# A Trainium2 kernel of two transformer blocks: the experts' outputs added to rows of x in DRAM by accumulating scatters

## The chip, the cores and the metric

The kernel runs on one core of one Trainium2 chip. The metric is the device time of one launch in microseconds (us); lower is better. Everything is float32 with float32-level accuracy: each product of a weight and an activation is made of three matrix multiplications of split operands (a rounded high part and the rest, the low part).

## The reference

Two blocks over one sequence of 512 tokens of width 1024. The first block is a mixer of three branches and then a hierarchical mixture of experts; the second block is attention, convolution, a memory attention and a feed-forward net. What is touched here is the end of the first block:

```python
def hier_moe(h, ...):                       # h: norm of x, 512 x 1024
    grp_prob = softmax(hf @ w_group + b_group);  p_g, g_idx = top_k(grp_prob, 1)      # 1 of 4 groups
    top_vals, e_idx = top_k(sel_logits, 2)                                            # 2 of its 4 experts
    weights = p_g * softmax(top_vals)
    for each expert e:  act = silu(hf @ w_gate[e]) * (hf @ w_up[e]) * combine[:, e];  y += act @ w_down[e]
x = x + gt2 * ffn        # end of the first block; the second block starts with rmsnorm(x)
```

So each token adds two experts' outputs, each times its own weight, to its row of x. There are 16 experts of hidden width 256.

## The kernel before

The tokens lie in four tiles of 128 (NT = 4). A planner holds all weight loads in the order of their use (`add_unit`, `fetch`): a load on SP's queue fills one of six raw buffers, ACT casts it to the high part, DVE (in the expert loop also Pool for some) subtracts to get the low part (`split_raw`, L212 and L215). A compiler pass orders the instructions of each engine and sets every semaphore; it also waits wherever two accesses to one tile, in DRAM too, must keep their order. Pages are 13 buffers of 128 x 2048 floats, shared by everything large.

*Up to the routing.* `wo_route` ends the mixer: it adds its output to x tile by tile, computes the norm for the experts, stores it to DRAM (`h2_d`, L1314) and computes the router's logits. x stays on the chip in two pages. Long before, `mixer` stores zeros to the last six of 24 blocks of `y_d` (L1224 to L1227).

*Routing.* `route` finds for each token its two experts, its two weights (`w12`) and its place: tokens of one expert get consecutive slots of a unit of 128 slots. There are 24 units; 18 are always worked on (one for each of 16 experts, two more for the experts that have over 128 tokens), six are spare. Matrix multiplications with one-hot operands turn places into a table that says which token sits in each slot of each unit (`slots`, L1515; empty slots name token 0), and `rowi` (L1497) says for each token at which rows of `y_d` its two outputs will lie.

*The expert loop.* `moe` visits the 18 units. For a unit, `gather` fetches 128 rows of `h2_d` by an indirect DMA on Pool's queue (L1532) into one of two buffers, TensorE transposes them (L1538), `expert_up` multiplies by the gate and up weights, `expert_down` by the down weights; a unit's `expert_down` stands in the program behind the next unit's `expert_up`. The result leaves PSUM on DVE, times the row gt2 (L1583, two halves of 128 x 512), into small buffers (tag `tmp`, five of them, used for other steps too), and SP stores each half to the unit's block of `y_d` (L1584).

*The branch.* Behind the 18 units stands a conditional (L1625) with the six spare units, which these inputs do not need. Each engine evaluates the branch; the queues of an engine whose DMAs were skipped bring their semaphores to the counts that the body would have left.

*The seam.* Eight indirect DMAs on Pool gather from `y_d` by token, 128 rows of 4 KB each, two for each tile of tokens (L1648). DVE multiplies each by its weight and adds it to x (L1652). After two tiles `fm_half` transposes x (L1715), scales it to the high and low parts (L1718, L1719) and computes the norm's factors (L1722 to L1731); then the other two tiles follow. Pool stores x to `x_d` (L1658); the second block loads it again from there some 250 us later (L2188). `self.mark`, the last L1652, is what two kinds of SP loads wait for at the start of the second block (the bias tables, L496, and one weight load, L183).

## Time and profile before

| | us |
|---|---|
| median of 3 runs | 1646.08 |
| lowest, highest | 1641.83, 1646.18 |
| the profiled execution, whole | 1647.19 |
| its span in the profile | 1645.2 |

The profile is of one execution. Busy shares of its span: TensorE 93%, DVE 64%, ACT 40%, Pool 16%. Its mean granted TensorE clock is 0.965 of full speed. A stretch's row tells the engines' busy time, the granted clock (1.00 is 2.4 GHz, 0.50 is 1.2 GHz) and the mean share of time in which the 16 DMA engines were busy. A row of waits names the waiting engine, the tile and the line, what ended the wait, the total, how often, and the longest. SyncE (SP) computes nothing, it issues DMAs.

### The profile page before, as it was taken

The page shows a single profiled execution, that of the slowest core. Times are in us where ns is not written, and L with a number is a line of the kernel's source. Part 1 is how long each engine was busy: PE and PEld are TensorE (multiplying, and loading weights), DVE is VectorE, ACT ScalarE, POOL GpSimd, SP SyncE. Part 2 cuts the span into 40 slices and gives each one's busy share as a digit, 9 for nine tenths or more (in the row PEclk, how much of TensorE's full clock was granted, in tenths as well). Part 3 has the DMA queues.
Part 4 walks back from the last instruction along what each step waited for, and adds up shares of the span by engine and source line. Part 5 has one row for each costly group of instructions (what it writes and reads, how often), then busy time and mean ns, then how long its engine had stood idle before and what let it go on. Part 6 is the DMA issues. An engine that isn't in the chain of part 4 may idle for free. (4 is left out here: it accounts for less than half of the span.)

```text
span 1645.2 us, 23279 instructions
## 1 busy us (share of the span) xinstructions
PE 1529.7 (93%) x8945; PEld 1289.3 (78%) x8945; DVE 1051.3 (64%) x2068; ACT 666.1 (40%) x1221; POOL 270.7 (16%) x294
## 2 busy tenths in 40 slices
PE   4999989999999999699985999999988999999998
PEld 3878867779988899588884886666766889889888
DVE  6797778755664466788986667777466541443445
ACT  6443434212342353555763444445455332331222
POOL 4032123110010000333323112112111110100010
PEclk9899999989999999799997989999999999999999
DMA  9334236324353324799995440113220223223221
GB/s 342 82 100 139 62 118 226 105 90 154 126 182 105 100 77 140 268 322 333 343 373 194 153 130 26 31 47 78 102 84 32 95 85 103 87 93 103 82 79 71
DMA packets 184118, 224.75 MB, mean 137 GB/s; under 512 B 11049, under 2 KB 161269, under 8 KB 184002
## 3 DMA queue, kind: packets, MB, share of 16 engines
q1 hardware_dynamic: 172432, 194.44, 35.7%
q0 software_dynamic: 7024, 26.48, 4.8%
q10 hardware_dynamic: 4546, 2.27, 0.6%
q8 instruction: 73, 1.20, 0.3%
q14 instruction: 43, 0.35, 0.1%
HBM read 204.27 MB, written 22.84 MB: 138 GB/s over the span
## 5 line engine op out<-in xcount | busy, mean ns | idle before, releaser
L238 PE MATMUL mm<-pg,whi 128*128 128x512 f32 (+1 forms) x968 | 380.6, 394 | 4.6 <-DVE pg L725 4.5
L239 PE MATMUL mm<-pg,whi 128*128 128x512 f32 (+1 forms) x968 | 379.0, 392 | 0.6 <-DVE pg L643 0.3
L240 PE MATMUL mm<-pg,wlo 128*128 128x512 f32 (+1 forms) x968 | 377.8, 391 | 0.0
L215 DVE TENSOR_TENSOR wlo<-wraw,whi 128x1024 fp32r<-128x1024 f32 (+3 forms) x204 | 239.6, 1186 | 211.0 <-ACT whi L212 209.9
L212 ACT CAST whi<-wraw 128x1024 fp32r<-128x1024 f32 (+3 forms) x210 | 200.2, 968 | 217.6 <-PE mm L239 119.9
L238 PE MATMUL mm<-whi,pg 128*128 128x256 f32 (+2 forms) x928 | 276.4, 298 | 6.4 <-ACT pg L857 3.1
L240 PE MATMUL mm<-whi,pg 128*128 128x256 f32 (+2 forms) x928 | 272.5, 294 | 0.0
L239 PE MATMUL mm<-wlo,pg 128*128 128x256 f32 (+2 forms) x928 | 272.3, 294 | 0.0
L238 PEld LDWEIGHTS mm<-pg,whi 128*128 128x128 f32 x968 | 185.5, 192 | 45.7 <-DVE pg L725 4.7
L239 PEld LDWEIGHTS mm<-pg,whi 128*128 128x128 f32 x968 | 185.7, 192 | 39.7 <-issue 2.1
L240 PEld LDWEIGHTS mm<-pg,wlo 128*128 128x128 f32 x968 | 185.9, 192 | 38.1 <-DVE wlo L215 0.8
L238 PEld LDWEIGHTS mm<-whi,pg 128*128 128x128 f32 x928 | 176.0, 190 | 13.5 <-ACT pg L857 3.3
L240 PEld LDWEIGHTS mm<-whi,pg 128*128 128x128 f32 x928 | 175.9, 190 | 4.7 <-DVE pg L274 0.6
L239 PEld LDWEIGHTS mm<-wlo,pg 128*128 128x128 f32 x928 | 176.1, 190 | 3.7
L2272 POOL TENSOR_TENSOR tmp<-tmp,bc 128x512 f32<-128x512 f32 x22 | 28.6, 1298 | 298.5 <-DVE tmp L2271 298.5
L436 DVE SCALAR_TENSOR_TENSOR tmp<-wraw,cact,tmp 128x256 f32<-128x256 f32 x112 | 57.0, 510 | 1.8
L2021 ACT ACTIVATE atmp<-atmp,nm 128x384 f32<-128x384 f32 (+3 forms) x64 | 34.9, 546 | 36.2 <-DVE nm L2019 25.0
L212 ACT CAST whi<-pg 128x1024 fp32r<-128x1024 f32 x36 | 36.3, 1052 | 19.0 <-PE mm L240 13.2
L239 PE MATMUL at<-wlo,pg 128*128 128x256 f32 x136 | 40.4, 297 | 3.6 <-DVE wlo L215 3.6
L238 PE MATMUL at<-pg,pg 128*128 128x256 f32 x152 | 43.7, 287 | 0.0
L215 DVE TENSOR_TENSOR wlo<-pg,whi 128x1024 fp32r<-128x1024 f32 x28 | 42.0, 1514 | 2.6 <-ACT whi L212 2.6
L239 PE MATMUL at<-pg,pg 128*128 128x256 f32 x152 | 43.3, 285 | 0.0
(557 smaller groups left out, 2632.1 us busy)
## 6 DMA issues: line engine op xcount, KB each, us to landing
wraw<-in_w_in_dram SPq DMA_DIRECT2D x34, 1024.0 KB
wraw<-in_w_mod_dram SPq DMA_DIRECT2D x16, 1024.0 KB
pg<-in_w_exp_gate_dram SPq DMA_DIRECT2D x14, 1024.0 KB
wraw<-in_ffn_wg_dram SPq DMA_DIRECT2D x11, 1024.0 KB
wraw<-in_ffn_wu_dram SPq DMA_DIRECT2D x11, 1024.0 KB
pg<-in_w_exp_down_dram SPq DMA_DIRECT2D x10, 1024.0 KB
y_d<-tmp SPq DMA_DIRECT2D x36, 256.0 KB
pg<-in_w_mod_dram SPq DMA_DIRECT2D x8, 1024.0 KB
```

The source lines that it names most:

```text
L212: cp = nc.scalar.copy(h, x)
L215: ins = eng.tensor_tensor(l, x, h.bitcast(F32), op=OP.subtract)
L238: nc.tensor.matmul(out, ah, bh, start=start, stop=False)
L239: nc.tensor.matmul(out, ah, bl, start=False, stop=False)
L240: nc.tensor.matmul(out, al, bh, start=False, stop=stop)
L436: nc.vector.scalar_tensor_tensor(t, w[:, k, :], self.cact[:, k:k + 1], t, op0=OP.mult, op1=OP.add)
L2021: nc.scalar.activation(lg[:, :n], lg[:, :n], AF.Exp, bias=nm, scale=-1.0, accum_out=den[:, c:c + 1])
L2272: nc.gpsimd.tensor_tensor(act[c], act[c], bc, op=OP.mult)
```

## The change

Six edits:

1. The zero stores and `y_d` go.
2. `wo_route` stores x, tile by tile on SP, to `x_d` before it stores the norm; the pages of x are given up there.
3. `route` keeps its eight one-hot tables in one page and uses them twice: for the token of each slot (now numbered from 1, so that 0 is an empty slot) and for the weight of each slot (`wslot`). From the former come `slots` as before and `dest`, the row of x for each slot, or a row beyond the end for an empty slot. `rowi` goes.
4. `expert_down` multiplies by gt2 and by the slot's weight in one operation per half, into one of two halves of a page (`yrows`), and one indirect DMA on Pool adds the 128 rows to the rows `dest` of `x_d`; rows beyond the end are skipped. Stores by SP go. The spare units do the same.
5. At the seam the gathers, the sums on DVE and Pool's store of x go. x is loaded from `x_d` on SP into two pages, and both calls of `fm_half` follow.
6. `self.mark` becomes the first L1719 operation of the second `fm_half`.

```diff
--- before.py
+++ after.py
@@ -1220,11 +1220,6 @@
         if not GFIRST:
             ya = self.gmlp(h, gc)
         self.gla_proj(h)
-
-        zero = self.t(self.lvp, [128, 1024], tag="lv")
-        nc.gpsimd.memset(zero, 0.0)
-        for u in range(18, NU):
-            nc.sync.dma_start(self.y_d[u * 128:(u + 1) * 128, :], zero)
         self.drain_bg()
         self.bg.append(self.gla_levels())
         self.pump(GP0)
@@ -1311,7 +1306,10 @@
             r = self.rstd(self.small, s1, D, 1, "rs2")
             nc.vector.scalar_tensor_tensor(self.L[:, i, :], pl[:, :20], r, self.br, op0=OP.mult, op1=OP.add)
             nc.vector.scalar_tensor_tensor(xs[i], xs[i], r, self.sh2r, op0=OP.mult, op1=OP.add)
+            nc.sync.dma_start(self.x_d[i * 128:(i + 1) * 128, :], self.x[i])
             nc.sync.dma_start(self.h2_d[i * 128:(i + 1) * 128, :], xs[i])
+
+        self.x = None
 
 
     def eid_value(self, table, u):
@@ -1335,11 +1333,15 @@
 
         self.iof, self.tok = iof[:, 0:128], iof[:, 128:132]
 
+        nc.vector.tensor_scalar(self.tok, self.tok, 1.0, None, op0=OP.add)
+
+        self.none = self.t(const, [128, 1], tag="none")
+        nc.vector.tensor_scalar(self.none, iof[:, 128:129], float(S), None, op0=OP.add)
+
         self.stri = self.t(const, [128, 128], tag="stri")
         nc.gpsimd.affine_select(out=self.stri, in_=self.ones, pattern=[[1, 128]], compare_op=OP.is_gt,
                                 fill=0.0, base=0, channel_multiplier=-1)
         self.h2_d = self.dram.tile([S, D], F32, name="h2_d")
-        self.y_d = self.dram.tile([128 * NU, D], F32, name="y_d")
         self.x_d = self.dram.tile([S, D], F32, name="x_d")
 
     def first_max(self, x, m, rev, out, shape):
@@ -1402,8 +1404,8 @@
         d = T("dd", NT)
         nc.vector.tensor_tensor(d, m2, m1, op=OP.subtract)
         nc.scalar.activation(d, d, AF.Exp)
-        self.w12 = self.t(self.const, [128, 2, NT], tag="w12")
-        w1, w2 = self.w12[:, 0], self.w12[:, 1]
+        w12 = T("w12", 2, NT)
+        w1, w2 = w12[:, 0], w12[:, 1]
         nc.vector.tensor_scalar(w1, d, 2.0, 2.0, op0=OP.mult, op1=OP.add)
         nc.vector.reciprocal(w1, w1)
         nc.vector.tensor_tensor(w1, w1, pg_, op=OP.mult)
@@ -1493,8 +1495,6 @@
             t = T("pick", NT, 16)
             nc.vector.tensor_tensor(t, O[c], unit, op=OP.mult)
             nc.vector.tensor_reduce(uc[:, c, :], t, axis=AX.X, op=OP.add)
-        self.rowi = self.t(self.const, [128, 2, NT], I32, tag="rowi")
-        nc.vector.scalar_tensor_tensor(self.rowi, uc, 128.0, sc_, op0=OP.mult, op1=OP.add)
 
         pt = self.ms()
         U4 = [128, 2, NT, 24]
@@ -1504,15 +1504,27 @@
         nc.vector.tensor_tensor(onu, uc.unsqueeze(3).to_broadcast(U4),
                                 self.iof[:, :24].unsqueeze(1).unsqueeze(1).to_broadcast(U4), op=OP.is_equal)
         nc.vector.tensor_tensor(tou, onu, self.tok.unsqueeze(1).unsqueeze(3).to_broadcast(U4), op=OP.mult)
+        Rp = self.page(F32R)
         for c in range(2):
             for i in range(NT):
-                R = self.t(self.small, [128, 512], F32R, tag="atmp", bufs=NATMP)
-                at, to = R[:, :128], tou[:, c, i, :]
+                q = NT * c + i
+                at, to = Rp[:, q * 128:q * 128 + 128], tou[:, c, i, :]
                 (nc.gpsimd if c < RP else nc.vector).tensor_scalar(at, self.iof, sc_[:, c, i:i + 1], None, op0=OP.is_equal)
-                q = NT * c + i
                 nc.tensor.matmul(pt[:, :24], at, to, start=q == 0, stop=q == 2 * NT - 1)
         self.slots = self.t(self.const, [128, NU], I32, tag="slots")
-        self.routed = nc.vector.tensor_copy(self.slots, pt[:, :NU])
+        self.routed = nc.vector.tensor_scalar(self.slots, pt[:, :NU], 1.0, 1.0, op0=OP.max, op1=OP.subtract)
+
+        dest = T("dest", NU)
+        self.after(nc.vector.tensor_scalar(dest, pt[:, :NU], 0.0, self.none, op0=OP.is_equal, op1=OP.mult), self.routed)
+        self.dest = self.t(self.const, [128, NU], I32, tag="dest")
+        nc.vector.scalar_tensor_tensor(self.dest, pt[:, :NU], -1.0, dest, op0=OP.add, op1=OP.add)
+        nc.vector.tensor_tensor(onu, onu, w12.unsqueeze(3).to_broadcast(U4), op=OP.mult)
+        pw = self.at()
+        for q in range(2 * NT):
+            nc.tensor.matmul(pw[:, :NU], Rp[:, q * 128:q * 128 + 128].bitcast(F32), onu[:, q // NT, q % NT, :], start=q == 0,
+                             stop=q == 2 * NT - 1)
+        self.wslot = self.t(self.const, [128, NU], tag="wslot")
+        nc.vector.tensor_copy(self.wslot, pw[:, :NU])
 
         eid = T("eid", 8)
         ef = T("ef", 6, 16)
@@ -1573,15 +1585,16 @@
         aT = self.t(self.small, [128, 512], F32R, tag="tmp", bufs=NTMP)
         self.split(aT[:, :256], aT[:, 256:], pt[:, :256])
         wh, wl = get("xd")
+        y = self.yrows[u % 2]
         for half in range(2):
             py = self.mm()
             hs = slice(half * 512, half * 512 + 512)
             for k in range(2):
                 self.mm3(py, aT[:, k * 128:(k + 1) * 128], aT[:, 256 + k * 128:256 + (k + 1) * 128],
                          wh[:, k, hs], wl[:, k, hs], k == 0, k == 1)
-            y = self.tmp()
-            nc.vector.tensor_tensor(y, py, self.gt2r[:, hs], op=OP.mult)
-            nc.sync.dma_start(self.y_d[u * 128:(u + 1) * 128, hs], y)
+            nc.vector.scalar_tensor_tensor(y[:, hs], py, self.wslot[:, u:u + 1], self.gt2r[:, hs], op0=OP.mult, op1=OP.mult)
+        nc.gpsimd.indirect_dma_start(out=self.x_d, out_offset=bass.IndirectOffsetOnAxis(ap=self.dest[:, u:u + 1], axis=0),
+                                     in_=y, in_offset=None, bounds_check=S - 1, oob_is_err=False, compute_op=OP.add)
 
     def moe(self):
         nc, tc, A = self.nc, self.tc, self.A
@@ -1590,6 +1603,8 @@
         self.ahead, self.limit = RAW + 2, self.order[("xd", UNITS[-1][1])] + LIM
         self.hold = self.routed
         self.mem_branch(*self.mem)
+        yp = self.page()
+        self.yrows = yp[:, :D], yp[:, D:]
         hT = self.gather(UNITS[0][0])
         self.hold = None
         uses, live = self.moe_order(), {}
@@ -1642,20 +1657,11 @@
                 self.expert_down(u, self.expert_up(self.gather(u, hroom), get), get)
         self.rooms = self.limit = None
         self.fm_begin()
-        pgs = [self.page() for _ in range(NT)]
-        for i in range(NT):
-            for c in range(2):
-                nc.gpsimd.indirect_dma_start(out=pgs[i][:, c * D:c * D + D], out_offset=None, in_=self.y_d,
-                                             in_offset=bass.IndirectOffsetOnAxis(ap=self.rowi[:, c, i:i + 1], axis=0))
-        for i in range(NT):
-            for c in range(2):
-                self.mark = nc.vector.scalar_tensor_tensor(self.x[i], pgs[i][:, c * D:c * D + D], self.w12[:, c, i:i + 1],
-                                                           self.x[i], op0=OP.mult, op1=OP.add)
-            if i % 2:
-                self.fm_half(self.nrm[0], i // 2, [pg[:, :D] for pg in pgs])
-
-        for i in range(NT):
-            nc.gpsimd.dma_start(self.x_d[i * 128:(i + 1) * 128, :], self.x[i])
+        self.x = self.load_x(nc.sync, self.x_d)
+        junk = self.tm_pages()
+        for hf in range(2):
+            self.mark = self.fm_half(self.nrm[0], hf, junk)
+
         self.x = None
 
 
@@ -1707,6 +1713,7 @@
 
         nc = self.nc
         hs = slice(hf * 256, hf * 256 + 256)
+        first = None
         for kk in range(4):
             pt = self.at() if kk % 2 else self.tp()
             for k in (2 * kk, 2 * kk + 1):
@@ -1716,8 +1723,9 @@
             for k in (2 * kk, 2 * kk + 1):
                 pk = pt[:, k % 2 * 256:k % 2 * 256 + 256]
                 nc.scalar.activation(self.fh[k][:, hs], pk, AF.Copy, scale=g[:, k:k + 1])
-                nc.vector.scalar_tensor_tensor(self.fl[k][:, hs], pk, g[:, k:k + 1], self.fh[k][:, hs].bitcast(F32),
-                                               op0=OP.mult, op1=OP.subtract)
+                q = nc.vector.scalar_tensor_tensor(self.fl[k][:, hs], pk, g[:, k:k + 1], self.fh[k][:, hs].bitcast(F32),
+                                                   op0=OP.mult, op1=OP.subtract)
+                first = first or q
         for i in (2 * hf, 2 * hf + 1):
             nc.scalar.activation(junk[i], self.x[i], AF.Square, accum_out=self.fms[:, i:i + 1])
         r = self.r[:, 2 * hf:2 * hf + 2]
@@ -1729,6 +1737,7 @@
             nc.vector.tensor_scalar(dg, self.ident, r[:, i:i + 1], None, op0=OP.mult)
             nc.tensor.matmul(pb[:, i * 128:(i + 1) * 128], self.ones, dg, start=True, stop=True)
         nc.scalar.copy(self.bc[:, hs], pb[:, :256])
+        return first
 
     def f2_halves(self, unit, evac):
 
```

## Rows read from the trace of the kernel before

**Rows 1.** Stretches: length, busy us of PE, PEld, DVE, ACT, POOL, clock, DMA, GB/s.
```profile
660.00:700.00 40.00, 23.83 (x163) 22.52 (x162) 31.55 (x81) 20.39 (x27) 12.50 (x8) 0.79 0.78 266
...
740.00:780.00 40.00, 37.89 (x266) 34.24 (x265) 33.80 (x43) 23.22 (x34) 13.16 (x7) 1.00 0.96 333
780.00:820.00 40.00, 38.32 (x269) 34.64 (x268) 38.56 (x48) 29.15 (x39) 13.19 (x8) 1.00 0.96 337
820.00:860.00 40.00, 37.23 (x260) 33.65 (x258) 34.22 (x41) 25.01 (x35) 12.20 (x5) 1.00 1.03 377
860.00:878.00 18.00, 13.94 (x73) 11.65 (x73) 13.61 (x16) 8.69 (x12) 3.10 (x2) 0.91 0.40 134
878.00:894.50 16.50, 0.00 (x0) 0.00 (x0) 6.20 (x7) 0.07 (x1) 6.47 (x7) 0.63 0.70 226
...
897.00:903.00 6.00, 6.00 (x29) 6.00 (x30) 5.08 (x9) 4.39 (x10) 2.11 (x4) 0.52 0.95 370
...
909.00:913.00 4.00, 3.43 (x26) 2.95 (x25) 3.84 (x11) 2.18 (x6) 2.77 (x6) 1.00 1.03 399
```

**Rows 2.** Waits, 640 to 930 us: engine, line, releaser: total us, times, longest.
```profile
POOL lv L1532 <- PE tp L1538: 88.0, 16, 9.2
...
PE tp L1715 <- DVE pg L1652: 18.0, 2, 16.6
...
PE tp L1538 <- DMA lv<-h_d,slots: 8.7, 2, 7.2
...
PE mm L240 <- DVE tmp L274: 7.6, 7, 2.0
...
ACT whi L212 <- DMA pg<-in_w_exp_gate_dram: 3.0, 1, 3.0
...
ACT pg L212 <- DMA pg<-in_w_exp_gate_dram: 2.3, 1, 2.3
```

**Rows 3.** Chain that ended last, around the seam: start us, length us, what.
```profile
885.50 0.70 issue
886.20 5.57 DMA pg<-y_d,rowi
...
895.63 1.30 DVE pg L1652
...
896.97 0.90 PE tp L1715 x3
```

**Rows 4.** Timeline of the seam: start us, length us, engine, line, operation.
```profile
877.97 1.29 DVE L1583 TENSOR_TENSOR tmp<-mm,pg 128x512 f32<-128x512 f32 x2
...
880.56 5.25 SPq L179 DMA_DIRECT2D wraw<-in_w_in_dram  x2
...
894.55 0.44 PE L1715 MATMUL tp<-ident,pg 128*128 128x128 f32 x1 [16.62 <-DVE pg L1652]
```

**Rows 5.** Instructions of the branch, L1625: ns min/median/max, first and last start us.
```profile
L1625 SPq EVENT_SEMAPHORE  x9: 17/17/17, 881.5 to 885.4; - x9
...
L1625 POOLq INC_SWDGE_SEM  x1: 762/762/762, 872.8 to 872.8; - x1
```

**Rows 6.** Instructions on `y_d`; below, the eight gathers' time to landing, 876 to 900 us.
```profile
L1584 SPq DMA_DIRECT2D y_d<-tmp x36: 319/344/2318, 702.9 to 879.3; - x36
...
DMA to landing us min/median/max: 5.5/5.7/6.0
```

**Rows 7.** Instructions of L1532, the loop's gathers, and their time to landing.
```profile
L1532 POOL DMA_INDIRECT lv<-h_d,slots x18: 936/958/2035, 670.4 to 829.2; - x18
...
DMA to landing us min/median/max: 4.1/7.0/8.8
```

**Rows 8.** All eight DMAs on `x_d`, stores and loads from Pool's queue: time to landing.
```profile
DMA to landing us min/median/max: 3.8/4.5/6.8
```

**Rows 9.** Issues of loads of x by SP, at the kernel's start, L714.
```profile
L714 SPq DMA_DIRECT2D pg<-in_x_dram x4: 393/428/438, 0.8 to 2.2; - x4
```

**Rows 10.** SP's own waits, 640 to 930 us.
```profile
SPq L1584 <- DVE tmp L1583: 82.1, 35, 10.0
```

## The prediction

> **What bounds the kernel now.** Read the stretches first [rows 1]. Before the experts, and again from 897 us on, TensorE is busy nearly all the time, so what the change does there (no zero stores, another store of x) can only cost. Two stretches are open. One is the routing, 660 to 700 us, where TensorE is busy for 23.83 of 40 us. The other is the seam between the experts and the second block: from 878.0 to 894.5 us TensorE does nothing, and restarts at the lower of its two clocks (granted 0.52 up to 903 us, 1.2 of 2.4 GHz). Between them, in the expert loop, TensorE is busy for 37 to 38.3 of each 40 us and the DMA engines for 0.96 to 1.03: two resources near their limit at once. The table of waits says who ends TensorE's idle time: 16.6 us at the seam end with the sum on DVE, L1652; 7.2 us in the routing end with the first gather; in the loop some 7.6 us in seven pieces end with DVE's split, L274, and ACT's casts of gate weights wait for a load by 5.3 us in two pieces only [rows 2].
>
> The seam is then read in order of time. The last two products of the last unit are scaled by 879.3 us (877.97 + 1.29) [rows 4]. Their stores land, SP closes the branch around the spare units with nine semaphore instructions up to 885.4 us [rows 5], the first gather starts at 886.20 and lands 5.57 us later, DVE adds tile after tile at 1.30 us, and the second tile of x, the first that completes a transposed pair, is ready at 896.93 (895.63 + 1.30) [rows 3]. TensorE had touched x[0] alone at 894.55 [rows 4]. So the seam is a chain of latencies: store, branch, gather, sum.
>
> **The change part by part.** I go by the profiled execution: 1647.19 us for a span of 1645.2. It lies 1.1 us above the median, 1646.08.
>
> *The seam.* Chain after: DVE scales the last half by 879.3; Pool issues one accumulating scatter, say at 879.4; it lands after L; Pool then closes its side of the branch, one increment of 0.76 us [rows 5]; SP issues the loads of x, 0.43 us each [rows 9]; x[1] is the second of them, and a load from x_d lands after 4.5 us in the median [rows 8]; 0.5 us I allow for the hand-overs (the chain shows 0.70 us of issue at one of them, rows 3). That is 879.4 + L + 0.8 + 0.9 + 4.5 + 0.5 = 886.1 + L. No accumulating DMA is in the trace, so L is bounded by its neighbours. From below by the quickest plain transfer on this queue with x_d, 3.8 us [rows 8]; from above by a read and a write in sequence, 8.8 us for the slowest gather under load [rows 7] and the median 4.5 us of x_d, 13.3 us. I take 7.5 us, near the gathers (5.5 to 6.0 us at this place [rows 6], 7.0 in the loop [rows 7]), since the scatter is the same kind of instruction, carries fewer rows (512 tokens times 2 experts in 18 units are 57 rows on average, of 128), but reads and writes each. Then x[1] is there at 893.6 instead of 896.93: -3.3 us. At the lower end the scatter isn't what ends last: SP is held until 885.4 and issues a load that is queued there [rows 4, 5], 0.4 us, then x: 885.4 + 0.4 + 0.9 + 4.5 + 0.5 = 891.7, so -5.2 us is the floor. At the upper end 899.4, +2.5 us.
>
> What DVE no longer adds, eight times 1.30 us, lay partly on this chain (the first four are in the number above); the other four lie at 902 to 907 us, beside a TensorE that is busy throughout [rows 1], and are worth only the 0.57 us that TensorE idles between 909 and 913 us. Sum of the seam -3.9 us, from -5.8 to +2.5. The low clock after the pause costs the same in both by this reckoning, as the pause is still over 13 us long; no row tells how it would follow a shorter one.
>
> The Trainium skill, in "DMA: Bandwidth & Descriptors" (section "Anatomy of one DMA — SWDGE (gpsimd) path"), fits such a DMA by 2.0 us and its bytes at 436 GB/s: an estimate of 3.2 us for 512 KB. The trace has 5.5 to 6.0 us for a gather of this size [rows 6]; the rows decide. By the page's figure the floor above would hold, -5.2 us.
>
> *The loop, DVE.* The 36 multiplications of 0.65 us by the gain row become 36 with a scalar more. An operation of that form with two tensors took 1.30 us for 1024 columns [rows 3], so 0.65 for 512: nothing.
>
> *The loop, SP and buffers.* 36 stores leave SP, where they waited 82.1 us in total for DVE with weight loads queued behind [rows 10]. The products go to a page of their own instead of two of five small buffers. The casts hardly waited for weights, so the first is worth about nothing, from 0 to -5.3 us; the second may shorten the splits' waits, 0 to -7.6 us [rows 2]. I take 0: these waits name DVE, which is busy 34 to 38.6 of 40 us, and it loses no work here.
>
> *The loop, Pool.* 18 scatters of 0.94 to 2.0 us each, like the gathers [rows 7], 17 to 36 us on an engine that is busy 13 of 40 us. Each waits for DVE's second half and for the scatter before it (both change x_d). Queued behind it on Pool are the next gather and a quarter or so of the weight splits; TensorE waits for both. The gather has cover: Pool itself waited 88.0 us for its buffer [rows 2], and it lands within 8.8 us [rows 7] of a unit's 10.3 us (36 stores from 702.9 to 879.3 us [rows 6], 17 periods). A delay of up to 2 us is hidden; I take 0, and +1 us per unit, 17 us, is the price if it isn't.
>
> *The loop, DMA.* Gone: 36 stores of 256 KB, 9.4 MB, 28 us of all engines at 333 GB/s [rows 1]. New: 1024 rows of 4 KB, 4.2 MB, 13 us if a row costs as much as a plain one, 38 us if it costs three times that (two reads and a write one after the other); plus 2.1 MB, 6 us, for storing x, which begins before 660 us where the DMA engines have room. Net -9 to +16 us of DMA time. Cover: 0.04 of the loop's 160 us, 6 us, and the lead at its end, where the engines are busy for 0.40 of 18 us [rows 1], 11 us. So I take 0.
>
> *Routing.* Out: one small DVE operation on the way to the slot table. New ones behind it (two of table size, one multiplication, eight small matmuls, a copy, under 2 us) fall into the 7.2 us in which TensorE awaits the first gather [rows 2]. 0, at most +1.
>
> Sum: -3.9 us, 1643.3 us for the profiled execution's counterpart, and 1.1 less against the median: 1642 us.
>
> **The rivals.**
> *Fast.* The scatter lands early and the seam comes to its floor, -5.8, and the freed buffers take half of the 7.6 us: -9.6 us, 1636 to 1637. For it: nothing but small buffers stands between some of these products. Against: DVE's load.
>
> *Slow, a chain of scatters.* Each scatter waits for its predecessor's landing. The point from which this decides is L = 10.3 us, the unit's period: beyond it Pool falls behind by L - 10.3 per unit, the page for the products (two units deep) fills, DVE can't empty PSUM, and TensorE waits at L's pace. At L = 11.5 that is 17 times 1.2, +20 us, with the seam at about 0: 1667; at 11.0, +12: 1658. For it: gathers already take up to 8.8 us beside the weights [rows 7] and only write or read. Against: on average less than half the rows. The Trainium skill has this as a rule (same page, "Rules for kernel authors"): an accumulate may lose another write of the same bytes that lands in between, so wait for the earlier DMA's semaphore. No run here shows a lost write; the wait's price is the one above.
>
> *Slow, DMA time.* A row costs three times a plain one, or the 57 rows fall to half of the engines, which no row of the trace tells: then a loaded engine has 25 to 76 us where the stores took 28, with x's 6 us a net +3 to +54, less the 17 us of cover: 0 to +37, by my choice +12. Weights come late, TensorE waits for them: 1654.
>
> *The seam doesn't shrink.* The reload waits for more than the last scatter (the branch, a page): +2 us, 1648.
>
> **How the numbers follow.** This kernel's measurement can tell about 0.3%, 5 us, from no change: faster is below 1641.1, slower above 1651.0. Forecast 0.40, of it 0.05 below 1641; fast 0.27; chain 0.17, of it 0.03 too small to see; DMA time 0.12, of it 0.02; seam 0.04, half of it slower by something else. So faster 0.32, same 0.42, slower 0.26. The range goes from 1633 (fast, with the splits' waits gone) to 1660 (chain at 11.1 us); the likeliest case's own is 1640 to 1649.
>
> **What would show it.** Right: TensorE restarts near 892 to 893 us by the old clock of the seam, with x[0] and x[1] together and no DVE sum ahead; the scatter lands in 6 to 9 us; no wait of Pool for a scatter; the loop from 700 to 878 as long as before. Chain: Pool's scatters wait for scatters, DVE's scaling for them, units at an even pace above 10.3 us. DMA time: weight casts of ACT that wait for loads. Wrong altogether, if the loop's length moves by more than 5 us without one of these, or the time before 660 us does.

## The result and the profile after

The changed kernel takes 1666.38 us in the median (1664.19 to 1671.92), against 1646.13 us (1641.83 to 1648.91) for the kernel before beside it: ratio 1.0135, 95% interval 1.0105 to 1.0166. It is slower by 1.35%, where 1642 us and no visible change were forecast; the time lies above the range's upper end of 1660 us. A second measurement gave 1663.61 against 1647.94 us, ratio 1.0105 (1.005 to 1.016).

The profiled execution after has a span of 1662.5 us, 17.3 more than before. I cut both spans at three places: the start of the first gather of the expert loop, the end of the last scaling of y (for before, [rows 7] and [rows 4] give them: 670.4 and 879.3), and the restart of TensorE behind the seam.

| us | before | after | difference | second profile of after |
|---|---|---|---|---|
| start to first gather | 670.4 | 677.2 | +6.9 | 673.9 |
| expert loop | 208.9 | 224.6 | +15.7 | 228.0 |
| seam, to TensorE's restart | 15.3 | 14.0 | -1.3 | 13.3 |
| from there to the end | 750.7 | 746.7 | -4.0 | 744.4 |

So the seam and what stands behind it became 5.3 us shorter, and the loop, where nothing was forecast, 15.7 us longer. The 6.9 us at the start are taken up at the end of the experiments.

The stretches of the loop in the changed kernel (columns as in [rows 1]):

```profile
740.00:780.00 40.00, 36.11 (x260) 33.28 (x259) 33.18 (x39) 24.01 (x32) 19.08 (x12) 1.00 0.95 307
780.00:820.00 40.00, 34.72 (x231) 31.00 (x230) 35.50 (x41) 23.77 (x33) 14.62 (x9) 0.96 0.90 278
820.00:860.00 40.00, 34.25 (x215) 30.66 (x216) 37.64 (x39) 23.13 (x30) 15.91 (x9) 0.91 0.94 306
```

TensorE is busy for 34.3 to 36.1 of 40 us instead of 37.2 to 38.3 [rows 1], and the granted clock, 1.00 throughout before, falls below it in two of the three. The DMA engines are busy for less, 0.90 to 0.95 instead of 0.96 to 1.03: they are not what became slow. The waits of the changed kernel, 640 to 930 us, say who makes TensorE idle (columns as in [rows 2]):

```profile
PE mm L240 <- DVE tmp L274: 24.0, 14, 3.2
...
PE tp L1722 <- DMA pg<-x_d: 14.8, 1, 14.8
...
POOL x_d L1596 <- DVE pg L1595: 10.8, 3, 8.9
...
POOL x_d L1596 <- DMA x_d<-pg,dest: 5.3, 1, 5.3
...
DVE pg L1595 <- DMA x_d<-pg,dest: 2.3, 1, 2.3
```

The wait for DVE's split of the activations (L274) has gone from 7.6 us in seven pieces [rows 2] to 24.0 in fourteen. A scatter waited for another scatter once in the loop, DVE for a scatter once. One unit of the loop, in the timeline (start us, length us, engine, line, operation), Pool first, then DVE, then TensorE:

```profile
810.46 0.99 POOL L1544 DMA_INDIRECT lv<-h_d,slots  x1 [7.22 <-PE tp L1550]
811.75 1.81 POOL L1596 DMA_INDIRECT x_d<-pg,dest  x1 [0.30 <-ACT pg L273]
813.01 3.00 POOL L215 TENSOR_TENSOR wlo<-pg,whi 128x1024 fp32r<-128x1024 f32 x1
...
812.61 6.76 DVE L215 TENSOR_TENSOR pg<-pg,pg 128x1024 fp32r<-128x1024 f32 x3
...
819.62 0.41 DVE L274 TENSOR_TENSOR tmp<-tp,tmp 128x256 fp32r<-128x256 f32 x1
...
820.09 0.79 PE L240 MATMUL mm<-whi,tmp 128*128 128x512 f32 x1 [2.34 <-DVE tmp L274]
```

A unit of the kernel before, with the same work:

```profile
796.90 0.94 POOL L1532 DMA_INDIRECT lv<-h_d,slots  x1 [8.08 <-PE tp L1538]
797.86 2.87 POOL L215 TENSOR_TENSOR wlo<-pg,whi 128x1024 fp32r<-128x1024 f32 x1
...
799.00 5.08 DVE L215 TENSOR_TENSOR pg<-pg,pg 128x1024 fp32r<-128x1024 f32 x3
```

Before, Pool's share of the split of the weights follows the gather at once; 1.73 us of it (799.00 to 800.73) lie beside DVE's three shares, which take 5.08 us. After, the scatter stands between the two, the share starts 2.55 us after the gather instead of 0.96, all 3.00 us of it lie beside DVE's three shares, and these take 6.76 us. Alone one of them takes 1.22 us (below), so three 3.66: DVE lost 1.4 us beside 1.73 us of Pool's share and 3.1 beside 3.00. At these two places DVE, in effect, stands while Pool's share runs. The activations' split queued behind comes late, TensorE waits 2.34 us for it, and the granted clock then falls, as the same place shows in windows of 4 us:

```profile
812.00:816.00 4.00, 4.00 (x37) 4.00 (x36) 4.00 (x3) 3.01 (x5) 4.00 (x2) 1.00 1.09 364
816.00:820.00 4.00, 1.75 (x10) 1.20 (x7) 4.00 (x6) 1.69 (x3) 0.00 (x1) 1.00 1.05 374
820.00:824.00 4.00, 3.91 (x13) 3.14 (x14) 3.09 (x6) 1.05 (x1) 0.00 (x0) 0.57 1.08 360
```

TensorE is busy for 1.75 of 4 us, and the next 4 us are granted at 0.57 of 2.4 GHz, nearly all at the lower level: another 1.7 us of its work lost (4 times 0.43). Most of the longer stalls cost twice in this way; one of 2.33 us, up to 763.2 us, didn't. From 720 to 860 us four windows of 20 us stand at 0.91 in the profile after and none before; 0.09 of 20 us is 1.8 us each.

The unit shown is no exception. At twelve of the fourteen waits for L274 in the changed kernel, the shares of DVE that start in the 9 us before the wait ends take together 1.6 to 3.3 us longer than alone, beside Pool's share; of the other two, one follows the wait of DVE for a scatter. Over the whole loop, before and after:

```profile
670.40:879.26 208.86, 185.59 (x1260) 168.13 (x1260) 179.39 (x212) 125.08 (x168) 67.11 (x34) 0.95 0.89 312
677.20:901.83 224.63, 195.87 (x1274) 175.85 (x1274) 197.31 (x216) 125.93 (x168) 91.05 (x51) 0.93 0.86 273
```

TensorE is idle for 28.8 us instead of 23.3, only 5.5 more: the 16.4 us more of waits for L274 are in part set off by shorter ones elsewhere, those for the first gathers above all (8.7 us [rows 2], now 2.1). The other 10.3 us of the loop's growth stand as busy time, for nearly the same products; the four windows at 0.91 make up some 7 of them. So the slower clock behind the stalls is a large part of the loss.

The Trainium skill has this port in "SBUF — State Buffer": by its section "Who interferes with whom" a DVE instruction with two SBUF inputs contends with a GpSimd instruction that reads SBUF, and by its section "Terms" the loser blocks rather than shares. The trace agrees: 3.1 us lost beside 3.00.

### The profile page after: what moved, and what is told of

The parts are those of the page before. It is cut to its first block, busy times and chain, and to the rows that moved or that the text cites. A ratio compares the mean times of both kernels' runs of the same rounds, so it can differ in the third digit from the quotient of the medians.

```text
span 1662.5 us, 23235 instructions
## 1 busy us (share of the span) xinstructions
PE 1538.6 (93%) x8961; PEld 1295.6 (78%) x8961; DVE 1058.4 (64%) x2065; ACT 666.5 (40%) x1221; POOL 289.0 (17%) x299
## 5 line engine op out<-in xcount | busy, mean ns | idle before, releaser
L215 DVE TENSOR_TENSOR wlo<-wraw,whi 128x1024 fp32r<-128x1024 f32 (+3 forms) x204 | 245.3, 1213 | 214.7 <-ACT whi L212 213.4
L238 PE MATMUL at<-pg,pg 128*128 128x256 f32 x152 | 43.8, 288 | 0.0
L240 PE MATMUL at<-pg,pg 128*128 128x256 f32 x152 | 43.4, 286 | 0.0
L239 PE MATMUL at<-pg,pg 128*128 128x256 f32 x152 | 43.2, 285 | 0.0
```

The costliest lines, as they stand in the source:

```text
L215: ins = eng.tensor_tensor(l, x, h.bitcast(F32), op=OP.subtract)
L238: nc.tensor.matmul(out, ah, bh, start=start, stop=False)
L239: nc.tensor.matmul(out, ah, bl, start=False, stop=False)
L240: nc.tensor.matmul(out, al, bh, start=False, stop=stop)
```

## Experiments

Three theories stood against one another. **A**: the scatter stands in Pool's queue ahead of Pool's share of the weights' split, which then falls on DVE's shares. **B**: the additions' transfers hold up the weights. **C**: a scatter holds up the next one, or the half of a page that it reads comes free too late. (In the expectation for e1_store the letter C stands for something else, the rest of the change; and the first expectations count the changed kernel's loop otherwise, as 227 us.) All runs together, the loop from the first gather to the last scaling, and TensorE's waits for the split L274 between 640 and 930 us:

| kernel | median us | ratio to before (95%) | loop us | waits us (times) |
|---|---|---|---|---|
| before | 1646.13 | | 208.9 | 7.6 (7) |
| after | 1666.38 | 1.0135 (1.0105 to 1.0166) | 224.6 | 24.0 (14) |
| after_again | 1663.61 | 1.0105 (1.005 to 1.016) | 228.0 | 24.4 (14) |
| e1_store | 1641.39 | 0.9954 (0.9928 to 0.9979) | 214.5 | 6.2 (6) |
| e2_plain | 1649.66 | 1.0012 (0.9982 to 1.0042) | 217.9 | 20.0 (14) |
| e5_zero | 1659.44 | 1.008 (1.0047 to 1.0113) | 226.4 | 23.9 (12) |
| e6_late | 1644.64 | 0.9977 (0.9956 to 0.9998) | 212.3 | 13.9 (11) |
| e3_after_dve | 1642.45 | 0.9968 (0.994 to 0.9995) | 205.6 | 5.9 (3) |
| e4_before_dve | 1627.55 | 0.9882 (0.9827 to 0.9938) | 194.7 | 0.9 (2) |
| e8_four | 1650.47 | 1.0012 (0.9984 to 1.0039) | 222.5 | 21.8 (11) |
| e8_again | 1651.29 | 1.0054 (1.0023 to 1.0086) | 218.2 | 19.3 (11) |
| e11_alternate | 1652.49 | 1.0036 (1.0007 to 1.0066) | 224.7 | 21.2 (12) |
| e9_four_dve | 1634.43 | 0.993 (0.9901 to 0.996) | 200.7 | 0.8 (2) |
| e12_alternate_dve | 1640.21 | 0.996 (0.9934 to 0.9987) | 201.2 | 1.9 (2) |
| e10_late_dve | 1635.39 | 0.9951 (0.9926 to 0.9976) | 201.8 | 1.3 (1) |
| e7_before_poolstore | 1651.69 | 1.0035 (1.001 to 1.006) | 207.8 | 13.5 (11) |

The kernel before, measured beside each, had medians of 1644.79 to 1647.94 us.

**e1_store: a store by place on SP instead of the scatter.**

```diff
-        nc.gpsimd.indirect_dma_start(out=self.x_d, out_offset=..., in_=y, ..., compute_op=OP.add)
+        nc.sync.dma_start(self.y_d[u * 128:(u + 1) * 128, :], y)
```

> The changed kernel with the scatter of each unit replaced by one plain store of its 128 x 1024 products by SP into a scratch in DRAM; the experts' outputs are left out of x. Theory A (Pool: the scatter's issue pushes Pool's weight split behind it, there the split holds up DVE's splits, and TensorE waits for DVE): without any scatter on Pool the loop, 227 us from the first gather to the last product in the changed kernel, comes back to about 209 us, and the whole to about 1646. Theory B (DMA time of the additions): the same loop, since these go too. Theory C (the rest of the change, such as the new page order or the multiplication by the slot's weight, makes the loop long): it stays near 225 us. The seam should be at its floor, as the load of x waits for no scatter.

The time is 0.46% below the kernel before, the waits for L274 are back at 6.2 us, and TensorE restarts 7.0 us after the last scaling. So the loss comes with the scatter. The rest of the change (the slot's weight, x in DRAM, one page for y) isn't free in the loop, which stays 5.6 us above before in this one profile: ACT's casts wait 12.3 us for loads of weights between 700 and 880 us, against 2.6 in the kernel before (700 to 870). The short seam hides that in the total. The longest of these waits in e1_store:

```profile
ACT whi L212 <- DMA pg<-in_w_exp_gate_dram: 3.7, 2, 2.5
ACT whi L212 <- DMA pg<-in_w_exp_down_dram: 2.5, 1, 2.5
ACT pg L212 <- DMA pg<-in_w_exp_gate_dram: 1.6, 2, 1.3
```

**e2_plain: the same scatters without the addition.**

```diff
-                                     in_=y, ..., oob_is_err=False, compute_op=OP.add)
+                                     in_=y, ..., oob_is_err=False)
```

> The changed kernel with the same scatters, which write their rows over those of x instead of adding to them; so the sum over two experts and x is left out. Theory A: Pool issues the same instructions, so the loop stays within 3 us of 227. Theory B: an addition reads and writes each row; without it the loop is 10 us or more shorter, near 212. The landing of a scatter tells what the addition costs: 6.8 us in the median with it; 5 to 6 without by B's reckoning.

Loop 217.9 us, 6.7 less than after, with 20.0 us of waits: the order on Pool is the same and the waits nearly so, but each scatter occupies Pool for less (median 1122 against 1706 ns) and lands sooner (5.0 against 7.3 us). Neither number came: theory A had wanted the loop within 3 us, theory B 10 us or more below. The length of the issue on Pool may count, and not its place alone; this run shortens the landing as well and doesn't part the two.

```profile
L1596 POOL DMA_INDIRECT x_d<-pg,dest x18: 975/1122/1807, 694.1 to 880.4; - x18
...
DMA to landing us min/median/max: 3.3/5.0/9.9
```

The rows are those of the scatter in e2_plain (ns min/median/max, first and last start), which leaves out the sum over two experts and x. In the changed kernel they read:

```profile
L1596 POOL DMA_INDIRECT x_d<-pg,dest x18: 1565/1706/2383, 709.1 to 904.5; - x18
...
DMA to landing us min/median/max: 5.0/7.3/9.4
```

**e5_zero: the changed kernel with `y_d` and the zero stores kept.**

```diff
+        zero = self.t(self.lvp, [128, 1024], tag="lv")
+        nc.gpsimd.memset(zero, 0.0)
+        for u in range(18, NU):
+            nc.sync.dma_start(self.y_d[u * 128:(u + 1) * 128, :], zero)
```

> The changed kernel with the zero stores kept: the old buffer of 24 blocks stands in DRAM again and its last six blocks are filled at about 250 us as before. In the changed kernel's profile the first 60 us took some 6 us longer than before, with the same instructions in the same order. If the place of the tensors in DRAM (one buffer of 12.6 MB less) makes the first loads slow, the first 160 us come back by 6 us and the whole to about 1660; if it is chance of single executions, the whole stays at 1664 to 1672 and the first 160 us differ from execution to execution.

Loop 226.4 us, as after: the zero stores have no part in it. Its first gather came at 664.1 us, so its profile shows no late start; its median of 1659.44 us, near the 1660 expected if the place in DRAM matters, is 4 to 7 us below the two of after: the start's question (below).

**e6_late: each scatter emitted one unit later.** Four halves of two pages for y, taken in turn.

```diff
     def expert_down(self, u, a, get):
         nc = self.nc
+        self.scatter()                     # of the unit before, if one is pending
...
-        y = self.yrows[u % 2]
+        y = self.yrows[self.turn % 4]
+        self.turn += 1
...
-        nc.gpsimd.indirect_dma_start(out=self.x_d, ...)
+        self.pending = (u, y)
```

> The changed kernel with each scatter put behind the next unit's up projections in the program, from four halves of two pages in turn; nothing is left out. Theory A: Pool's weight split goes ahead of the scatter again, DVE is held up as little as before, and the loop comes back to 209 to 213 us; the whole to about 1650. Theory B: the same rows are added, the loop stays near 227. If Pool's own time is what counts (18 scatters of 1.7 us), and not its order, the loop stays near 225 too.

1644.64 us, ratio 0.9977: 19 to 22 us below the two medians of after, with the same additions, the same bytes and the same rows. Theory B in its plain form falls here. In this trace the share can follow the gather again, and three shares of DVE beside it then take as long as before the change (5.08 us there):

```profile
803.95 2.92 POOL L215 TENSOR_TENSOR wlo<-pg,whi 128x1024 fp32r<-128x1024 f32 x1
...
805.12 5.10 DVE L215 TENSOR_TENSOR pg<-pg,pg 128x1024 fp32r<-128x1024 f32 x3
```

The run changed two things at once, though, order and halves. The next ones part them.

**e3_after_dve and e4_before_dve: no share on Pool, in the changed kernel and in the one before.**

```diff
-PLO = 1
+PLO = 0
```

> The changed kernel with the split of the weights taken off Pool: all of it is on DVE (PLO = 0). To be read against the kernel before with the same edit, which runs beside it. Theory A (the scatter stands in Pool's queue ahead of Pool's share of the split of the weights, so that the share runs late, beside DVE's own shares, and DVE's split of the activations comes late at TensorE): with no share on Pool nothing is left there to be late, and the loop of the experts (first gather to the last scaling of y, 208.9 us before, 224.6 us in the changed kernel) is at most 5 us longer than in the kernel before with the same edit; waits of TensorE for DVE's split of the activations differ by under 6 us between the two. Theory B (the additions' time in the DMA engines): the loop stays 13 to 18 us longer than in its partner. Theory C (the scatters' two halves come free too late, or a chain of one scatter behind the other): also 10 us or more longer than its partner.

> The kernel before with the split of the weights taken off Pool (PLO = 0), the partner of the run above. DVE takes on 36 shares of 1.21 us each, some 44 us in all. If DVE has that room in the loop (it waits for weights there), the loop stays at 209 to 215 us; if it has not, it grows to 220 to 250 us, and then the difference to the partner is what is read, not the time itself. All theories agree on this run.

Two results. First, Pool's shares cost the kernel before as well: without them it takes 1627.55 us, ratio 0.9882, and its loop is 194.7 us, where 209 us or more had been expected. (It takes over 16 shares, not the 36 expected: between 660 and 910 us DVE does 100 of 128x1024, 84 in the kernel before.) DVE's share by itself takes 1.22 us; next to Pool's it took 1.37 in the kernel before and 1.56 after (groups of instructions of e4_before_dve, before, after: busy us, mean ns):

```profile
L215 DVE TENSOR_TENSOR pg<-pg,pg 128x1024 fp32r<-128x1024 f32 x32 | 38.3, 1222 | 0.7 <-ACT pg L212 0.7
```

```profile
L215 DVE TENSOR_TENSOR pg<-pg,pg 128x1024 fp32r<-128x1024 f32 x24 | 32.3, 1368 | 0.7 <-ACT pg L212 0.7
```

```profile
L215 DVE TENSOR_TENSOR pg<-pg,pg 128x1024 fp32r<-128x1024 f32 x24 | 36.9, 1558 | 0.7 <-ACT pg L212 0.7
```

In this form 32 shares at DVE's own pace take 38.3 us, hardly more than the 36.9 us that 24 of them take in the changed kernel while Pool does the other eight: the relief was none. Second, theory A's number was missed. The changed kernel's loop is still 10.9 us longer than its partner's (205.6 against 194.7), where at most 5 had been expected, and its median 14.9 us above (1642.45 against 1627.55). With Pool's shares gone from both kernels the change costs nearly what it costs with them (15.7 us in after_again); Pool's queue can't be the only way in which the scatters cost time. The waits for L274 are down to 5.9 us in three pieces, and in the trace of e3_after_dve the two long ones have another cause: DVE's scaling waits for the half of a page that a scatter still reads.

```profile
733.82 1.41 DVE L1595 SCALAR_TENSOR_TENSOR pg<-mm,wslot,pg 128x512 f32<-128x512 f32 x2 [3.31 <-DMA x_d<-pg,dest]
...
741.68 0.56 PE L240 MATMUL mm<-whi,tmp 128*128 128x512 f32 x1 [2.24 <-DVE tmp L274]
...
787.96 1.41 DVE L1595 SCALAR_TENSOR_TENSOR pg<-mm,wslot,pg 128x512 f32<-128x512 f32 x2 [4.15 <-DMA x_d<-pg,dest]
...
795.82 0.50 PE L240 MATMUL mm<-whi,tmp 128*128 128x512 f32 x1 [2.37 <-DVE tmp L274]
```

Both units last longer for it, 14.0 and 14.9 us from gather to gather instead of some 10, and at each the clock falls (0.75 and 0.83 from 740 to 748, 0.57 from 796 to 800 us). The half is chosen by the unit's number, and units 14, 16, 2 and 15, 17, 5 follow one another: three in a row use the same half. So C has a part as well.

**e8_four, e8_again and e11_alternate: other halves, scatters in place.** Four halves in turn in the first two, the same two halves in turn in the last.

```diff
-        y = self.yrows[u % 2]
+        y = self.yrows[self.turn % 4]      # e11_alternate: % 2
+        self.turn += 1
...
```

> The changed kernel with four halves of two pages for y, taken in turn, instead of two by the unit's number; the scatters stay where they are. It parts the two things that the late scatter did at once. Theory A (order on Pool): the loop stays near the changed kernel's 224.6 us, at most 4 us shorter, and the time is 1655 to 1664 us. Theory C (the halves came free too late, above all where three units in a row use the same one): the loop comes to 210 to 216 us, and the time to 1643 to 1650 us.

> The changed kernel with four halves again. Its ten times lay 1644 to 1660 us and its profile, at the upper end, showed the changed kernel's long loop (222.5 us): the long units come or stay away from one execution to the next. If so, the median is again 1646 to 1655 us, and a profile of an execution near the median has a loop of 208 to 216 us with fewer falls of the granted clock; if the loop is always long, the median comes out at 1656 to 1664 us.

> The changed kernel with its two halves for y used in turn instead of by the unit's number, a one-line edit: units 14, 16, 2 and 15, 17, 5 follow one another and share a half in the changed kernel. If the three in a row are what the four halves mended, this run comes out as they did: median 1646 to 1655 us, no wait of DVE for a scatter in the loop. If two halves are too few as such, it stays at 1658 to 1667 us with one or more such waits.

Medians of 1650.5, 1651.3 and 1652.5 us, 11 to 16 us below the two of after, and no wait of DVE for a scatter in any of the three loops. Beside Pool's shares two halves seem enough if they alternate; what they mended is the three in a row. Theory A's 1655 to 1664 us for e8_four were missed, and so were theory C's 210 to 216 us for its loop and the 208 to 216 us for that of e8_again. But the waits for L274 stay at 19 to 22 us: Pool's shares still come late, as A says. What isn't settled is the size. The three profiles show loops of 222.5, 218.2 and 224.7 us, 0 to 10 us below those of after, and two of the three are profiles of executions at the upper end of their times (1659.98 and 1663.27 us). The times of these kernels spread over 16 to 22 us; whether the loop or the start makes that spread can't be told from three profiles. What the order on Pool's queue costs by itself is the step from here to e6_late, which has the same four halves and the scatter later: 5.8 and 6.7 us in the medians, 10.2 and 5.9 in the loops.

**e9_four_dve, e12_alternate_dve and e10_late_dve: both causes gone.** PLO = 0 with four halves, with two in turn, and with four halves and the late scatter.

```diff
-PLO = 1
+PLO = 0
...
-        y = self.yrows[u % 2]
+        y = self.yrows[self.turn % 4]      # e12_alternate_dve: % 2
+        self.turn += 1
```

> The changed kernel with both causes taken away that the runs so far leave: no share of the split of the weights on Pool (PLO = 0), and four halves of two pages for y in turn. Theory A with C (Pool's late shares, and beside them a half of y that comes free only when a scatter has landed; together they are the whole loss in the loop): the loop, first gather to the last scaling of y, is 194 to 199 us (the kernel before with PLO = 0: 194.7; the changed one with PLO = 0 and two halves: 205.6, with two waits of DVE of 3.3 and 4.2 us for a half and two falls of the granted clock behind them); DVE's waits for scatters are gone; the time is 1623 to 1632 us. If something else of the scatters costs (their transfers, Pool's descriptors), the loop stays at 203 to 207 us and the time at 1636 to 1646 us.

> The same with no share of the split of the weights on Pool (PLO = 0). If the three units in a row were the whole of what two halves cost, the loop comes to 194 to 202 us as with four halves (200.7) and the time to 1629 to 1638 us; if not, the loop stays near 205.6 us and the time near 1642 us.

> The changed kernel with each scatter emitted at the start of the next unit's second part, four halves in turn, and no share of the split on Pool. If the place of the scatter in Pool's queue matters only through Pool's shares, this run and the one above (scatter not delayed) agree within 4 us in the loop and 6 us in time. If a scatter also delays the gather behind it so that TensorE waits for rows of h, this one is the faster by 5 us or more.

Loops of 200.7, 201.2 and 201.8 us; the waits for L274 are 0.8 to 1.9 us. A late scatter brings nothing more once Pool has no shares (1635.39 against 1634.43 us): its place mattered through the shares. All three are faster than the kernel before, and 7 to 13 us slower in the median than the kernel before with the same PLO. None of the times expected for e9_four_dve and e12_alternate_dve came: 1634.43 lies between the two ranges, and 1640.21 is near the "if not" of 1642 us, although the loop is in the range. With Pool's shares gone, alternating halves brought the median down by only 2.2 us from e3_after_dve's, four halves by 8.0; the loops of the two, 0.5 us apart, don't show why. The loop lies 6 us above that partner's 194.7, not within 194 to 199 as expected for e9_four_dve, and the 6 us are one unit, the last gap between gathers (16.7 us there, 10.6 in e4_before_dve). There the casts of the weights wait for loads (e9_four_dve, ACT, then windows of 2 us):

```profile
818.58 2.00 ACT L212 CAST whi<-pg 128x1024 fp32r<-128x1024 f32 x2 [2.27 <-DMA pg<-in_w_exp_up_dram]
822.50 1.05 ACT L212 CAST whi<-pg 128x1024 fp32r<-128x1024 f32 x1 [1.92 <-DMA pg<-in_w_exp_down_dram]
```

```profile
822.00:824.00 2.00, 0.00 (x0) 0.00 (x0) 0.14 (x1) 1.50 (x4) 0.00 (x0) 0.74 0.84 258
824.00:826.00 2.00, 1.86 (x4) 1.49 (x5) 2.00 (x5) 1.52 (x3) 0.00 (x0) 0.50 0.97 302
826.00:828.00 2.00, 2.00 (x11) 1.98 (x10) 1.22 (x2) 0.00 (x0) 0.00 (x0) 0.50 1.05 393
```

The DMA engines are busy throughout from 824 to 828 us (0.97 and 1.05), and TensorE's pause of some 3 us is followed by more than 5 us at the lower clock. Between 700 and 870 us the casts wait 13.9 us for loads in e9_four_dve and 0.3 us in e4_before_dve. It looks like theory B, where nothing else holds up the loop, but e1_store speaks against the additions as its cause: it has no scatter at all, and its casts wait 12.3 us for loads. What in the change makes the loads late stays open.

**e7_before_poolstore: the kernel before, its stores of y issued on Pool.**

```diff
-            nc.sync.dma_start(self.y_d[u * 128:(u + 1) * 128, hs], y)
+            nc.gpsimd.dma_start(self.y_d[u * 128:(u + 1) * 128, hs], y)
```

> The kernel before with its 36 stores of y issued on Pool's queue instead of SP's: no accumulation, no indices, the same bytes by place, and Pool's queue holds two issues per unit that wait for DVE's scaling, ahead of Pool's shares of the split. Theory A (order on Pool's queue): the loop grows from 208.9 us by 5 to 15 us, with Pool's shares later and more waits of TensorE for DVE's split of the activations than the 7 of the kernel before. Theory B (the scatters' own transfers): the loop stays within 3 us of 208.9.

Mixed. The time is 0.35% longer (0.1 to 0.6) and the waits for L274 rise from 7.6 to 13.5 us, in the direction of A. The loop of the profile isn't longer (207.8 us), which A had wanted. That profile is of the fastest of its executions (1644.48 us of 1644.48 to 1659.29); I take it as weak support and no more. Two issues of 0.56 us per unit are also less than one of 1.7.

**after_again, and the start.**

> The changed kernel itself, beside the same runs of the kernel before. Its profile of before showed the layer's start some 6 us late in a stretch in which both kernels do the same. If that was chance, the median here is 10 to 16 us over the kernel before and the difference from first gather to the restart of TensorE behind the seam stays at 12 to 16 us; if the change itself delays the start, the median is again 18 to 22 us over it.

The loss is there again, +15.7 us in the median, with a loop of 228.0 us and a start only 3.5 us late; from the first gather to TensorE's restart it is 17.1 us longer than before, where 12 to 16 had been expected. What comes before the first gather varies from one execution to the next, with the same or nearly the same instructions in all kernels: over 16 profiles the first gather starts between 662.3 and 679.3 us. One place that varies is 320 to 360 us. The two rows in the changed kernel, then in e2_plain:

```profile
320.00:340.00 20.00, 19.07 (x97) 15.36 (x95) 14.23 (x26) 3.25 (x4) 4.54 (x4) 0.80 0.26 81
340.00:360.00 20.00, 19.48 (x88) 15.06 (x86) 8.99 (x13) 4.42 (x5) 2.41 (x2) 0.86 0.31 104
```

```profile
320.00:340.00 20.00, 19.23 (x114) 15.76 (x115) 10.83 (x20) 5.38 (x7) 2.45 (x2) 1.00 0.25 80
340.00:360.00 20.00, 19.21 (x113) 15.03 (x112) 15.04 (x25) 2.39 (x4) 3.46 (x4) 1.00 0.37 122
```

The clock falls there in some executions and not in others; in the profile of before it does too (0.66 in the first of the two windows). Another is the first 60 us: the first copy of L772 by ACT starts at 59.7 us in the profile of before and at 64.5 in that of after, but at 59.9 in after_again, and at 63.5 and 63.7 in e4_before_dve and e7_before_poolstore, which do the same as before up to there. So 4.8 of the 6.9 us of the first comparison are a lateness that comes and goes in both kernels. Not settled is whether the change shifts the odds: the five profiles of kernels that still have `y_d` start the gather at 664.1 to 672.2 us, the eleven without it at 662.3 to 679.3, nine of them above 672.2.

## Why the prediction was wrong

**The step that failed is "The loop, Pool".** It named both things that queue behind the scatter, the next gather and a share of the weights' split, and it set a price aside: 1 us per unit, 17 us. The loop grew by 15.7 and 19.1 us; that the price fits so well is luck, as other causes have a part in that growth (below). The step gave the cover for the gather alone ("A delay of up to 2 us is hidden; I take 0") and none for the share. The gather was indeed covered: TensorE waited for it 2.1 us in the loop, and it lands within 8.1 us. The share had no cover. It was timed, by nothing but its place in the queue, to run for a good part beside operations of DVE that it doesn't disturb, and moving it by the scatter's 1.6 us set it beside those that it stops: TensorE's waits for the split of the activations rose from 7.6 to 24.0 us. The rows to see this were in the trace of before: DVE's three shares at 799.00 took 5.08 us instead of 3.66. (Pool does 16 of 100 shares of 128x1024 there, not a quarter.)

**The clock was left out.** The step priced a delay at its own length. In the changed kernel a stall of 2.3 us was followed by a stretch at the lower clock that cost another 1.7 us, and over the loop TensorE's busy time grew by more than its idle time (10.3 against 5.5 us). The forecast looked at the clock in the seam only.

**"The loop, SP and buffers" was wrong too.** It took a page of two halves to be no worse than five small buffers. The half was chosen by the unit's number while the units run out of order, and I didn't go through that order: three in a row share a half. Used in turn, the same two halves give 11 to 14 us back in the medians, four halves 12 to 16, an amount of which the profiles explain only a part: DVE waits for a scatter 2.3 us in after and 4.7 in after_again.

**How the loss divides stays open.** By the medians the halves are the larger part (11 to 16 us, and 6 to 7 for the order on Pool's queue); by the trace of after it is the queue, with twelve of the fourteen waits. And with Pool's shares taken from both kernels the change still costs 10.9 us in the loop, of which late loads and the shared half are what the traces show.

**The seam came out near the forecast, by other terms, and that is luck.** The working said: scaled at 879.3, one scatter 0.1 us later, 7.5 us to land and 0.8 for Pool's side of the branch, 5.9 us for the reload, together 14.3 us from the last scaling to TensorE's restart. It took 14.0. The timeline of the changed kernel's seam (the last scaling, the last two scatters, the loads of x, TensorE):

```profile
901.08 0.75 DVE L1595 SCALAR_TENSOR_TENSOR pg<-mm,wslot,pg 128x512 f32<-128x512 f32 x1 [0.17 <-PE mm L240]
...
897.74 1.56 POOL L1596 DMA_INDIRECT x_d<-pg,dest  x1 [8.93 <-DVE pg L1595]
904.50 1.57 POOL L1596 DMA_INDIRECT x_d<-pg,dest  x1 [5.19 <-issue]
...
911.92 1.77 SPq L714 DMA_DIRECT2D pg<-x_d  x4
...
915.81 0.45 PE L1722 MATMUL tp<-ident,pg 128*128 128x128 f32 x1 [14.77 <-DMA pg<-x_d]
```

The last scatter starts 2.7 us after the scaling ended at 901.83, not 0.1: Pool had nothing to do, and both scatters change x_d, so it waits for the one before. Its way to the loads of x took 7.4 us (8.3 forecast), the reload 3.9 (5.9). Errors of opposite sign; against [rows 4] the pause of TensorE is 1.3 us shorter. Without the scatters the seam is 7.0 us (e1_store), so the scatters' chain and landing are half of the 14.0, and the forecast's floor, 5.2 us below before, was no floor: e1_store is 8.3 us below.

Behind the restart the kernel gained 4.0 us more (6.3 in the second profile), where 0.57 were forecast and the low clock was to cost the same in both. It doesn't. The first 8 us behind the restart, before and after:

```profile
894.55:898.55 4.00, 2.66 (x12) 2.26 (x13) 3.52 (x3) 2.54 (x5) 1.78 (x3) 0.50 0.97 343
898.55:902.55 4.00, 4.00 (x20) 4.00 (x19) 3.52 (x8) 2.80 (x7) 1.92 (x3) 0.50 0.97 387
```

```profile
915.81:919.81 4.00, 3.91 (x21) 3.51 (x22) 1.21 (x3) 1.71 (x5) 0.00 (x0) 0.60 0.70 283
919.81:923.81 4.00, 4.00 (x36) 3.82 (x34) 2.22 (x6) 4.00 (x10) 0.30 (x2) 1.00 0.00 0
```

TensorE, with both halves of x there at once, is busier in these 8 us (7.91 instead of 6.66), and the granted clock is back at full speed some 4 us sooner. Up to the first L721 of ACT, 54.4 us behind the restart in before, both profiles of after gain 2.0 us; the other 2.0 and 4.3 come far behind it and may be chance.

**The rivals.** *A chain of scatters* would decide at L = 10.3 us; the scatters landed in 7.3 us in the median, 9.4 at most, and one waited for another once in the loop: not the cause, though its time (1667) came out. *DMA time*: the DMA engines were busy for less than before, and e6_late makes the same additions in 19 to 22 us less; casts wait for late loads only when the rest is taken away, and in e1_store without any addition. *Fast*: the freed buffers took nothing off the waits, they tripled. The rival that would have been right wasn't written down as one; it was a price within a step, set aside in half a sentence. The prediction's own test for being wrong altogether, a loop that moves by more than 5 us without a chain or late weights, was met; in the first profile the time before 660 us moved by more than 5 us too.

**Routing** held: from the last store of the norm to the first gather it takes 16.4 us before and 16.8 after.

## What to carry to other kernels

Before an instruction is put into a queue, list everything behind it in that queue, and ask of each not only whether someone waits for it, but what will run beside it on the other engines at its new time; here Pool's share of a split stopped shares of DVE for nearly as long as it ran. A buffer chosen by an item's number must be checked against the order in which the items are worked on. And a change that loses can show that the kernel before had the same loss already: taking Pool's shares away, with no scatters at all, is the fastest version here, 1627.55 us, 1.2% below the kernel before.

## What the runs showed of the hardware

- Pool's elementwise operation on SBUF can stop DVE's with two SBUF inputs: three shares of DVE took 6.76 us beside 3.00 us of Pool's share, 5.08 beside 1.73, and 1.22 us each alone. It isn't always DVE that loses: in the trace of before a share of DVE that started at 831.31 us took its 1.22 us although Pool's started 0.2 us later, and Pool's took 3.27 us instead of the 2.4 that it takes at 732.27, where no share of DVE meets it.
- The addition makes an indirect scatter dearer on Pool too, not only in transfer: 1706 against 1122 ns of Pool's time for 128 rows of 4 KB, empty slots among them, and 7.3 against 5.0 us to land.
- A pause of TensorE of 2 to 3 us inside a stretch at 2.4 GHz was, at most places, followed by 3.4 to more than 5 us at 1.2 GHz, in after (0.57 from 820 to 824 us), e3_after_dve (0.57 from 796 to 800) and e9_four_dve (0.50 from 824 to 828).
- Nearly the same instructions up to the first gather took 662.3 to 679.3 us over the 16 profiles, part of it a fall of the clock between 320 and 360 us that comes or stays away.
